# One store for the shift's last tokens, one page per unit, and stores moved to GpSimd's and ScalarE's queues

## The chip, the core and the metric

The kernel runs on one core of a Trainium2 chip. The metric is the device time of one execution, in microseconds (us). A core has TensorE (PE, with PEld for its weight loads), VectorE (DVE), ScalarE (ACT), GpSimd (POOL) and SyncE (SP). Each engine works through a queue of its own in order, and an instruction at the head of a queue that waits holds everything behind it. A DMA is issued by an instruction in the queue of SP, ACT or POOL and is then moved by 16 DMA engines, which all queues share.

## What is computed

One inference step of a hybrid decoder layer, for a prompt of 2048 new tokens and for 8 sampled sequences with 4096 cached positions each. After a modulated RMS norm, one projection makes the columns of two head groups. The first is sparse attention: an indexer scores all earlier positions, the best ones are attended. The second is RWKV-7 time mixing, whose columns pass a token shift before a delta-rule recurrence:

```
def rwkv_branch(xs, prev_row, S0, gate, mu_shift, ...):
    prev = jnp.concatenate([prev_row.astype(xs.dtype), xs[:, :-1]], axis=1)
    xm = xs + mu_shift * (prev - xs)
    r, k, v, wd, ad = jnp.split(xm, [...], axis=-1)
    ...
    S_new, y = wkv_scan(S0, rf, heads(decay), k_mod, vf, -kk, kk * a_h)
    ...
    return out.astype(xs.dtype), S_new, xs[:, -1:]
```

`xs[:, -1:]` is an output of its own, `shift_p`: the last token's 1664 projected columns, before the shift. The two groups' outputs are joined, projected once more and added to x. For the sampled sequences, the indexer's keys come from a paged cache: `cache_kidx[page_table]`, 32 pages of 128 positions for each of 8 sequences.

## The kernel before

The program is written against tiles in pools. A planner orders the instructions of all queues by a priority (the place in the program, shifted by `later(n)` by n places) and by a simulated timeline, allocates the buffers, and puts in every wait. `after(x, [y])` asks only that x stand behind y in that order. A tile with `bufs=1` has one buffer, so that its next user waits until every reader of the old content is done.

**Phase G** (`phase_g`) makes the projections of the prompt and runs the RWKV group. Tokens stand on the free axis in eight pieces of GT = 256. After a first part (norm, the "ad" columns in `g_ad`, the first gates in `g_ga`) comes a loop of 32 units k = (p, u): four pairs of heads p, eight token pieces u each. A unit passes through

- `front`: `g_front` multiplies the pair's columns r, k, v and gate (PE L196), copies them with scale to the tile `raw` (ACT L506) with one column for the token before, and mixes the shift (DVE L512). `raw` is a tile of 128 channels x 3 kinds x 257 columns with `bufs=1`; `g_pair` makes a new one for each pair and clears its column 0 (the memset of L489);
- `g_elem`: decays, keys and the like, on DVE and ACT;
- `g_chunk`: products within the pieces (L622, L627), then a round trip that turns small triangular blocks: eight stores asc<-UA (L643), eight loads As<-asc (L647), 15 steps of two GpSimd operations (L655, L656, Ut and Us), eight stores tsc<-Us (L658), one load TT<-tsc (L661);
- `g_inv` and `g_tail` take TT (first read by DVE L672), finish the inverse, run the recurrence (L770, L772), normalise, and store the result: ym is made by ACT (L813) and POOL (L814) and stored by SP to `mixd` (L815).

In iteration k the program has elem and chunk of unit k + 1, inv and tail of unit k, front of unit k + 2, then "filler" jobs (`a_job`, `g_ga`): matmuls that prepare the attention group (L204), whose queries are stored by SP from the tile `qo` (L872). Then `PG` steps of the generator `s_pages`, then `prefetch`, which loads the next weight tile (`load_w`: four loads wst of L178, each turned into two f16 halves by ACT L181 and DVE L182; `w` has four buffers) and, for some tiles, multiplies the sampled tokens' columns (`s_cols`), whose result `sat` is stored by SP (L341).

**The shift's last tokens.** The last column of `raw` after the last token piece is the output. In `g_front`, at u = 7, three stores (L518) write 128 floats each, one float from each partition; `g_ad` does so once (L469). That is 13 stores of 0.5 KB.

**The pages.** `s_pages` brings 32 groups of pages of the indexer's cache into a linear buffer `kxd`: an indirect gather issued by POOL (L1461) into the tile `pg` of 128 x 512 floats with `bufs=1`, and a store issued by SP (L1462). `PG = 2`: two of these steps per unit. `kxd` is read in phase A (`s_scores`, L1472).

**Phase A** (`phase_a`) loads K and V (L933, L934), scores, searches, attends and multiplies out, with the sampled sequences' work as background. Its instructions are in the same order plan; the loads have a priority of -3000.

Of the kernel before, what the change touches and what calls it, by code (L numbers as in the profile page):

```python
# [9 lines left out]
F32 = mybir.dt.float32  # L10
# [6 lines left out]
OP = mybir.AluOpType  # L17
# [14 lines left out]
GT = 256  # L32
# [8 lines left out]
class Kern:  # L41
# [166 lines left out]
    def phase_g(self):  # L208
        nc, V, A, G, PE, SY = self.nc, self.V, self.A, self.G, self.PE, self.SY
# [6 lines left out]
        with ExitStack() as es:  # L216
# [5 lines left out]
            bs = self.bs  # L222
# [24 lines left out]
            st, cx = {}, {}  # L247
# [55 lines left out]
            n = len(seq)  # L303
# [20 lines left out]
                prefetch()  # L324
            for _ in pages:
                pass
            self.A.activation(self.sg, self.sgr, AF.Tanh, scale=0.5)
            V.tensor_scalar(self.sg, self.sg, 0.5, 0.5, op0=OP.mult, op1=OP.add)
            V.tensor_tensor(self.sg, self.sg, self.sgr, op=OP.mult)

    def s_cols(self, name, w):

        c0 = {"q0": 0, "q1": 256, "kv": 512, "i0": 768, "i1": 1024, "ix": 1280}.get(name)
        if c0 is None:
            return
        ps = self.bank("e", 2)
        n = 72 if name == "ix" else 256
        self.gemm_n(ps[0:8, 0:n], self.hsl, w[:, :, :, 0:n])
        t = self.be.tile([8, 256], F32, name="sat", tag="bon", bufs=3)[:, 0:n]
        self.A.activation(t, ps[0:8, 0:n], AF.Copy, scale=1.0 / WS)  # L340
        self.SY.dma_start(self.sAd[:, c0:c0 + n], t)  # L341

    def gemm_u(self, u, w, dst):

# [15 lines left out]
    def consts_g(self, bs):  # L360
        V, SY = self.V, self.SY
        pb = self.pb
        P = lambda i: pb[:, 13 + 4 * i:17 + 4 * i]
        self.w0, self.a0, self.kk_w, self.ka, self.rk, self.lnw, self.lnb = (P(i) for i in range(7))
        dp = bs.tile([128, 5, 4], F32, name="dp")
        V.tensor_scalar(dp[:, 0], self.w0, 0.5, None, op0=OP.mult)
        V.tensor_scalar(dp[:, 1], self.a0, 0.5, None, op0=OP.mult)
        V.tensor_scalar(dp[:, 2], self.ka, 0.5, None, op0=OP.mult)
        V.tensor_scalar(dp[:, 3], self.ka, -0.5, 1.0, op0=OP.mult, op1=OP.add)
        V.tensor_scalar(dp[:, 4], self.kk_w, -0.5, None, op0=OP.mult)  # L370
        self.w0h, self.a0h, self.kah, self.kac, self.kkb = (dp[:, i] for i in range(5))

        self.RS = bs.tile([128, 2, 2, 2, 2], F32, name="RS")
        V.memset(self.RS, 1.0)
        self.omu = bs.tile([128, 13], F32, name="omu")
        V.tensor_scalar(self.omu, pb[:, 0:13], -1.0 / WS, 1.0 / WS, op0=OP.mult, op1=OP.add)

        self.lor = bs.tile([128, 4, 512], F16, name="lor")
        V.memset(self.lor[:, 2:4], 0.0)
        lo = self.a["lora"]  # L380
        for j in range(3):
            t = self.ap_.tile([128, 512], F32, name="lt", tag="nat", bufs=2)
            if j < 2:
                SY.dma_start(t, bass.AP(tensor=lo.tensor, offset=lo.offset + 64 * 512 * j, ap=[[0, 2], [512, 64], [1, 512]]))
            else:
                SY.dma_start(t, lo)
            if j < 2:
                self.A.activation(self.lor[:, j], t, AF.Copy, scale=WS)
                i = slice(64, 128)
                V.scalar_tensor_tensor(self.lor[i, j], t[i], WS, self.lor[i, j], op0=OP.mult, op1=OP.subtract)  # L390
            else:
                for n in range(2):
                    i = slice(64 * n, 64 * n + 64)
                    self.A.activation(self.lor[i, 2 + n], t[i], AF.Copy, scale=WS)

        self.wdad = self.dr.tile([128, 3, T], F16, name="wdad")
        self.raw12 = bs.tile([128, GT + 1], F32, name="raw12")
        V.memset(self.raw12[:, 0:1], 0.0)
        self.lwx = bs.tile([128, NCH, 65], F32, name="lwx")
        V.memset(self.lwx, 0.0)  # L400
        cg = bs.tile([128, CG_N], F32, name="cg")
        SY.dma_start(cg, self.a["cg"])
        self.cos = cg[:, 0:256].rearrange("p (i d) -> p i d", i=16)
        self.sin = cg[:, 256:512].rearrange("p (i d) -> p i d", i=16)
        self.wqk = bs.tile([128, 2, 64], F32, name="wqk")
        wq = self.a["wqk"]
        SY.dma_start(self.wqk.rearrange("p h d -> p (h d)"), bass.AP(tensor=wq.tensor, offset=wq.offset + 448, ap=[[0, 128], [1, 128]]))
# [41 lines left out]
    def g_ad(self, u, w):  # L449

        V, A, SY = self.V, self.A, self.SY
        sl = slice(u * GT, (u + 1) * GT)
        raw, out = self.raw12, self.be.tile([128, GT], F32, name="wo", tag="ta", bufs=1)
# [12 lines left out]
                SY.dma_start(self.wdad[64 * d:64 * d + 64, j, sl], hl[64 * j:64 * j + 64, 0])  # L466
        SY.dma_start(self.wdad[:, 2, sl], hl[:, 1])
        if u == T // GT - 1:
            SY.dma_start(self.a["o_shift_p"][12 * 128:13 * 128].rearrange("(p o) -> p o", o=1), raw[:, GT:])  # L469

    def g_ga(self, j, i, w):

# [19 lines left out]
    def g_front(self, st, u, w0, w1):  # L492
        nc, V, A, G, PE, SY = self.nc, self.V, self.A, self.G, self.PE, self.SY
        be = self.be
        p, raw = st["p"], st["raw"]
# [17 lines left out]
                if 2 * b + c0 + n == 4:  # L513
                    self.silu(gate, pg[:, (n - 1) * GT:])
        if u == T // GT - 1:
            for j in range(3):
                c0 = (4 * j + p) * 128
                SY.dma_start(self.a["o_shift_p"][c0:c0 + 128].rearrange("(p o) -> p o", o=1), raw[:, j, GT:])  # L518
        return dict(st=st, u=u, xm=xm, gate=gate, i=p * (T // GT) + u)

    def rsqrt(self, x):
# [86 lines left out]
    def g_chunk(self, cx):  # L608
# [20 lines left out]
        for s, src in ((2, BK.rearrange("p a s t -> p (a s) t")), (3, AV)):  # L629
            pt = self.bank("e", 2)  # L630
# [13 lines left out]
                         UA[16 * n:16 * n + 16, n // 4, :, :, 0, q:q + 16].rearrange("p a h t -> p (a h) t"))  # L644
        As = bv.tile([128, 16, 16], F32, name="As", bufs=2)
        for n in range(8):
            SY.dma_start(As[16 * n:16 * n + 16], bass.AP(tensor=asc.tensor, offset=asc.offset + 1024 * n,  # L647
                                                         ap=[[0, 4], [256, 4], [1, 256]]))
        Us = bv.tile([128, 4, 16], F32, name="Us", bufs=2)
        G.tensor_copy(Us, self.uinit)  # L650
# [1 line left out]
        for j in range(15):  # L652
            m, w = j // 4 + 1, 15 - j
            sh = [128, m, w]
            G.tensor_tensor(Ut[:, 0:m, j + 1:], bc(As[:, j:j + 1, j + 1:], sh), bc(Us[:, 0:m, j:j + 1], sh), op=OP.mult)  # L655
            G.tensor_tensor(Us[:, 0:m, j + 1:], Us[:, 0:m, j + 1:], Ut[:, 0:m, j + 1:], op=OP.add)  # L656
        for n in range(8):
            SY.dma_start(bass.AP(tensor=tsc.tensor, offset=tsc.offset + 16 * n * 256 + 16 * (n % 4),  # L658
                                 ap=[[256, 4], [64, 4], [1024, 4], [1, 16]]), Us[16 * n:16 * n + 16])
# [53 lines left out]
    def g_tail(self, cx):  # L713
# [98 lines left out]
        V.scalar_tensor_tensor(yc, yc, col(self.lnb), gate, op0=OP.add, op1=OP.mult)  # L812
        A.copy(ym[:, 0], yc)  # L813
        G.tensor_tensor(ym[:, 1], yc, ym[:, 0], op=OP.subtract)  # L814
        SY.dma_start(self.mixd[:, :, 4 + p, sl], ym)  # L815


    def a_job(self, kind, ip, w):
# [44 lines left out]
        if nh == 4:  # L863
# [5 lines left out]
            o = ap.tile([128, 2, 4, 128], F16, name="qo", tag="qo", bufs=2)  # L869
            A.copy(o.rearrange("p t h q -> p (t h q)"), pt)  # L870
            c = int(kind[1])
            SY.dma_start(self.qTd[kind[0] == "i"][:, 2 * ip:2 * ip + 2, 4 * c:4 * c + 4], o)  # L872
        else:
            if kind == "kv":
                SY.dma_start(tok(self.a["o_k_p"]), n3)
# [570 lines left out]
    def s_pages(self, p):  # L1446
# [11 lines left out]
        yield  # L1458
        for n in range(32):
            t = p.tile([128, 512], F32, name="pg", bufs=1)  # L1460
            G.indirect_dma_start(out=t, out_offset=None, in_=rows, in_offset=bass.IndirectOffsetOnAxis(ap=it[:, n:n + 1], axis=0))  # L1461
            SY.dma_start(self.kxd[n // 4, 8 * (n % 4):8 * (n % 4) + 8].rearrange("j (q d) k -> (j q) (d k)", q=16), t)  # L1462
            yield

    def s_scores(self, p):
        nc, V, A, G, PE, SY = self.nc, self.V, self.A, self.G, self.PE, self.SY
# [366 lines left out]
PB = 6  # L1833
P_LD = -3000
P_SC = 0
FILL = lambda k: 4 + (52 * (k + 1) + 28) // 29
F0, F1 = 1, 4
YB = 2
PG = 2
XTB, SQB = 3, 3  # L1840
X0 = 2
SQP = (0, 2)
# [217 lines left out]
```

## Time and profile before

| | us |
|---|---|
| median of 3 runs | 2457.18 |
| lowest, highest | 2455.85, 2461.61 |
| profiled execution | 2460.94 |
| its span, from first to last instruction | 2459.1 |
| unit loop, first asc store to last store of ym | 232.6 to 1464.1 |

The mean granted clock of TensorE is 0.925 of full speed. The chain of work that ended last is made up thus:

```profile
PE 33%; POOL 22%; DVE 11%; DMA 11%; issue 9%; SPq 7%; ACT 5%; POOLq 0%; DVEq 0%; ACTq 0%
```

A name with q is an engine's sequencer: an instruction that waits or issues a DMA while the engine proper does nothing. In the timeline, a row holds the start, the time taken, the engine, the line, the operation, the tiles written and read, the shapes, and in square brackets how long the engine had been idle and what ended that. In the list of waits a row holds who waited for what, the total, the times and the longest. In the view of one line, a row holds the count, then the shortest, median and longest duration in ns. SP only issues, so that its rows are issue times; where a DMA ends shows in who was released by it.

Two lists show what SP's own queue and POOL wait for most in the unit loop:

```profile
POOL Ut L655 <- DMA As<-asc: 217.7, 25, 23.2
```

```profile
SPq L658 <- POOL Us L656: 149.7, 28, 12.3
```

### The profile page before, as it was taken

The numbers are of one execution on the slowest core, as the hardware profiler recorded it, in microseconds if no ns is written. First come the engines' busy times: TensorE is split into PE (matmuls) and PEld (weight loads), VectorE is DVE, ScalarE is ACT, GpSimd is POOL, SyncE is SP. The second block draws the span as 40 slices with busy tenths as digits, with TensorE's granted clock in tenths as the row PEclk, the third lists the DMA queues.
The fourth block names the chain that finished last, engine by engine and source line by source line (L and its number), as shares of the span: only waits on it lengthen the run. The fifth ranks groups of instructions, "written<-read, shape, count | busy, mean of one in ns | idle before, by whom it ended". The sixth has DMA issues, their size and how long they took to land.

```text
span 2459.1 us, 55537 instructions
## 1 busy us (share of the span) xinstructions
PE 2108.7 (86%) x20799; PEld 1497.6 (61%) x20799; DVE 1611.1 (66%) x4998; ACT 1060.8 (43%) x2243; POOL 1097.0 (45%) x2841
## 2 busy tenths in 40 slices
PE   6788998699998999979998756998887789888997
PEld 1656777587776788868876432455555445455553
DVE  4883576586775766767876776867787744556531
ACT  1652223232332333322322345888767543665530
POOL 2311345334343243232343326357767765577722
PEclk9898999899999999989999676999889999998999
DMA  6435332311112211132111412312000033220133
GB/s 223 153 113 133 96 106 92 85 51 34 33 48 42 54 51 36 49 62 58 42 37 27 130 29 70 101 58 64 10 27 10 18 84 97 65 59 27 49 104 100
DMA packets 232537, 167.59 MB, mean 68 GB/s; under 512 B 108327, under 2 KB 193280, under 8 KB 232129
## 3 DMA queue, kind: packets, MB, share of 16 engines
q1 hardware_dynamic: 226817, 149.27, 21.8%
q0 software_dynamic: 3328, 10.49, 1.6%
q8 instruction: 165, 2.70, 0.5%
q10 hardware_dynamic: 2112, 4.19, 0.5%
q14 instruction: 115, 0.94, 0.1%
HBM read 113.87 MB, written 50.00 MB: 67 GB/s over the span
## 4 chain that ended last, share of the span: by engine, by line
PE 33%; POOL 22%; DVE 11%; DMA 11%; issue 9%; SPq 7%; ACT 5%; POOLq 0%; DVEq 0%; ACTq 0%
PE ps_g L196 8%; PE ps_s L1341 5%; SPq L647 3%; POOL Us L656 3%; POOL Ut L655 3%; PE ps_l L1031 3%; PE ps_v L1281 2%; PE ps_g L204 2%; PE ps_t L1273 2%; SPq L658 2%; PE ps_g L159 2%; ACT bias L1092 2%; DMA As<-asc 1%; DVE sc L1049 1%; PE ps_e L622 1%
## 5 line engine op out<-in xcount | busy, mean ns | idle before, releaser
L196 PE MATMUL ps_g<-h,w 128*128 128x256 f16 (+1 forms) x4032 | 512.0, 281 | 34.0 <-ACT sgr L356 8.1
L196 PEld LDWEIGHTS <-w 128*128 128x128 f16 x4032 | 394.7, 101 | 105.0 <-issue 31.2
L204 PE MATMUL ps_g<-w,h 128*128 128x256 f16 (+1 forms) x2304 | 251.8, 263 | 3.0 <-ACT nat L848 2.4
L655 POOL TENSOR_TENSOR Ut<-As,Us 128x12 f32<-128x12 f32 (+10 forms) x480 | 130.8, 273 | 260.1 <-DMA As<-asc 217.7
L1252 DVE CUSTOM_DVE_ANT_0 P<-ps_l,bias 128x1024 f32<-128x1024 f32 (+7 forms) x192 | 172.5, 908 | 106.2 <-PE ps_l L1031 61.4
L204 PEld LDWEIGHTS <-h 128*128 128x128 f16 (+1 forms) x2448 | 210.1, 99 | 35.9 <-issue 8.1
L1273 PE MATMUL ps_t<-cf,P 128*128 128x128 f32 x1088 | 185.3, 298 | 32.4 <-ACT P L1260 21.4
L1276 ACT COPY pT<-ps_t 128x512 f32<-128x512 f32 (+1 forms) x288 | 154.0, 560 | 128.7 <-PE ps_t L1273 125.3
L1049 DVE SCALAR_TENSOR_TENSOR sc<-r,wi,sc 128x1024 f32<-128x1024 f32 (+7 forms) x154 | 167.7, 1089 | 37.2 <-ACT r L1048 36.4
L1260 ACT ACTIVATE P<-P,mx 128x1024 f32<-128x1024 f32 (+7 forms) x192 | 171.5, 896 | 39.9 <-DVE mx L1258 39.6
L1273 PEld LDWEIGHTS ps_t<-cf,P 128*128 128x128 f32 x1088 | 130.0, 149 | 89.7 <-ACT P L1260 28.3
L1281 PE MATMUL ps_v<-pT,Vn 128*64 128x128 f32 x2176 | 162.7, 292 | 21.8 <-ACT pT L1276 21.2
L1341 PE MATMUL ps_s<-wo,mt 128*128 128x512 f16 x768 | 172.4, 379 | 7.8 <-DVE t L1345 6.3
L1048 ACT ACTIVATE r<-ps_l 128x1024 f32<-128x1024 f32 (+7 forms) x176 | 142.4, 816 | 76.4 <-PE ps_l L1031 48.5
L1031 PE MATMUL ps_l<-K,qiT 128*128 128x512 f16 (+3 forms) x608 | 154.9, 379 | 23.7 <-ACT r L1048 12.3
L1031 PE MATMUL ps_l<-K,qT 128*128 128x512 f16 (+3 forms) x640 | 155.4, 365 | 19.2 <-ACT r L1048 12.9
L1281 PEld LDWEIGHTS ps_v<-pT,Vn 128*64 128x64 f32 x2176 | 123.2, 143 | 70.3 <-ACT pT L1276 36.8
L1092 ACT ACTIVATE bias<-sc,sm 128x640 uint8<-128x640 f32 (+13 forms) x84 | 109.9, 1308 | 129.5 <-POOL sm L1123 113.3
L656 POOL TENSOR_TENSOR Us<-Us,Ut 128x12 f32<-128x12 f32 (+10 forms) x480 | 133.9, 279 | 34.7
L1341 PEld LDWEIGHTS <-mt 128*128 128x128 f16 x768 | 74.7, 98 | 96.0 <-issue 9.0
L1031 PEld LDWEIGHTS <-qT 128*128 128x128 f16 x640 | 64.7, 104 | 79.5 <-issue 40.8
L1031 PEld LDWEIGHTS <-qiT 128*128 128x128 f16 x608 | 61.6, 106 | 83.2 <-issue 48.9
(561 smaller groups left out, 4234.2 us busy)
## 6 DMA issues: line engine op xcount, KB each, us to landing
wst<-in_wt SPq DMA_DIRECT2D x60, 256.0 KB
xt<-in_xT SPq DMA_DIRECT2D x16, 512.0 KB
wa<-in_w_ada SPq DMA_DIRECT2D x8, 1024.0 KB
kxd<-pg SPq DMA_DIRECT2D x32, 256.0 KB
qTd<-qo SPq DMA_DIRECT2D x32, 256.0 KB
kx<-kxd SPq DMA_DIRECT2D x64, 128.0 KB
mt<-mixd SPq DMA_DIRECT2D x16, 512.0 KB
x<-in_x SPq DMA_DIRECT2D x32, 256.0 KB
```

The lines of the kernel that those rows point to most:

```text
L196: self.PE.matmul(out, w[:, a, k], h[:, b, k], start=(n == 0), stop=(n == 3 * KD - 1))
L204: self.PE.matmul(out, h[:, b, k], w[:, a, k], start=(n == 0), stop=(n == 3 * KD - 1))
L655: G.tensor_tensor(Ut[:, 0:m, j + 1:], bc(As[:, j:j + 1, j + 1:], sh), bc(Us[:, 0:m, j:j + 1], sh), op=OP.mult)
L656: G.tensor_tensor(Us[:, 0:m, j + 1:], Us[:, 0:m, j + 1:], Ut[:, 0:m, j + 1:], op=OP.add)
L1031: self.PE.matmul(ps[:, j:j + m], qs, self.K[:, kk, c0 + j:c0 + j + m], start=st, stop=not st)
L1049: self.dve = V.scalar_tensor_tensor(sc[:, c:c + n], r[:, :n], wi[:, h:h + 1], self.tz[:, c:c + n] if h == 0 else sc[:, c:c + n], op0=OP.mu ...
L1092: self.after(A.activation(ja[:, :L], sc[:, :L], AF.Sign, bias=t, accum_out=col(5)), [self.act])
L1252: self.dve = V.tensor_tensor_reduce(P[n][:, :w], pl[:, :w], bias[:, c:c + w], scale=1.0, scalar=-3.0e38, op0=OP.add, op1=OP.max, accum_out ...
L1260: self.act = A.activation(P[n][:, :w], P[n][:, :w], AF.Exp, scale=0.125, bias=mx[:, h, 2:3], accum_out=sums[:, n, h:h + 1])
L1273: PE.transpose(pt[:, q:q + 128], Ps[g][k // 8][:, k % 8 * 128:(k % 8 + 1) * 128], self.ident)
L1281: mm = PE.matmul(pv[64 * g:64 * g + 64, hh * 128:(hh + 1) * 128], self.Vn[:, k, 64 * g:64 * g + 64], pT[:, q + g * 128:q + g * 128 + 128], ...
L1341: PE.matmul(pg, mt[:, b, k], self.wo[:, a, k, js], start=(n == 0), stop=(n == 3 * KD - 1))
```

## The change

Four edits go together.

1. The 13 stores of single floats are replaced. A tile `shp` of 128 x 13 is filled by small DVE copies: one in `g_ad`, and one of three columns per pair in `g_front` (columns p, p + 4, p + 8). After the loop, with a priority moved 40 places ahead, a PE transpose turns it to 13 rows of 128, a DVE copy takes it to the tile `sho`, and one SP store writes 13 rows of 512 B.
2. `PG = 1`: one step of `s_pages` per unit. The gather must stand behind the last Us operation that has been written so far, the store of a page comes one step later and must stand behind the last As load written so far. The single buffer stays.
3. The store of `ym` is issued by POOL in place of SP.
4. The stores of `qo` and `sat` are issued by ACT in place of SP.

```diff
@@ phase_g, after the loop
             for _ in pages:
                 pass
+            with self.later(P_SH):
+                pt = self.bank("m", 2)
+                PE.transpose(pt[0:13, 0:128], self.shp, self.ident)
+                t = self.be.tile([13, 128], F32, name="sho", tag="So", bufs=1)
+                V.tensor_copy(t, pt[0:13, 0:128])
+                SY.dma_start(self.a["o_shift_p"].rearrange("(c p) -> c p", p=128), t)
@@ s_cols
-        self.SY.dma_start(self.sAd[:, c0:c0 + n], t)
+        self.A.dma_start(self.sAd[:, c0:c0 + n], t)
@@ consts_g
+        self.shp = bs.tile([128, 13], F32, name="shp")
@@ g_ad
         if u == T // GT - 1:
-            SY.dma_start(self.a["o_shift_p"][12 * 128:13 * 128].rearrange("(p o) -> p o", o=1), raw[:, GT:])
+            V.tensor_copy(self.shp[:, 12:13], raw[:, GT:])
@@ g_front
         if u == T // GT - 1:
-            for j in range(3):
-                c0 = (4 * j + p) * 128
-                SY.dma_start(self.a["o_shift_p"][c0:c0 + 128].rearrange("(p o) -> p o", o=1), raw[:, j, GT:])
+            V.tensor_copy(self.shp[:, p:p + 9:4], raw[:, :, GT])
@@ g_chunk
-            SY.dma_start(As[16 * n:16 * n + 16], ...
+            self.h_as = SY.dma_start(As[16 * n:16 * n + 16], ...
...
-            G.tensor_tensor(Us[:, 0:m, j + 1:], Us[:, 0:m, j + 1:], Ut[:, 0:m, j + 1:], op=OP.add)
+            self.h_us = G.tensor_tensor(Us[:, 0:m, j + 1:], Us[:, 0:m, j + 1:], Ut[:, 0:m, j + 1:], op=OP.add)
@@ g_tail
-        SY.dma_start(self.mixd[:, :, 4 + p, sl], ym)
+        G.dma_start(self.mixd[:, :, 4 + p, sl], ym)
@@ a_job
-            SY.dma_start(self.qTd[kind[0] == "i"][:, 2 * ip:2 * ip + 2, 4 * c:4 * c + 4], o)
+            A.dma_start(self.qTd[kind[0] == "i"][:, 2 * ip:2 * ip + 2, 4 * c:4 * c + 4], o)
@@ s_pages
         for n in range(32):
             t = p.tile([128, 512], F32, name="pg", bufs=1)
-            G.indirect_dma_start(out=t, ...)
-            SY.dma_start(self.kxd[...], t)
+            ld = G.indirect_dma_start(out=t, ...)
+            self.after(ld, [self.h_us])
             yield
+            st = SY.dma_start(self.kxd[...], t)
+            self.after(st, [self.h_as])
@@ constants
+P_SH = -40
-PG = 2
+PG = 1
```

More of the change, by code (lines that the diff above doesn't have):

```diff
@@ L646, in g_chunk @@
         for n in range(8):
-            SY.dma_start(As[16 * n:16 * n + 16], bass.AP(tensor=asc.tensor, offset=asc.offset + 1024 * n,
+            self.h_as = SY.dma_start(As[16 * n:16 * n + 16], bass.AP(tensor=asc.tensor, offset=asc.offset + 1024 * n,
                                                          ap=[[0, 4], [256, 4], [1, 256]]))
@@ L1460, in s_pages @@
             t = p.tile([128, 512], F32, name="pg", bufs=1)
-            G.indirect_dma_start(out=t, out_offset=None, in_=rows, in_offset=bass.IndirectOffsetOnAxis(ap=it[:, n:n + 1], axis=0))
-            SY.dma_start(self.kxd[n // 4, 8 * (n % 4):8 * (n % 4) + 8].rearrange("j (q d) k -> (j q) (d k)", q=16), t)
+            ld = G.indirect_dma_start(out=t, out_offset=None, in_=rows, in_offset=bass.IndirectOffsetOnAxis(ap=it[:, n:n + 1], axis=0))
+            self.after(ld, [self.h_us])
             yield
+            st = SY.dma_start(self.kxd[n // 4, 8 * (n % 4):8 * (n % 4) + 8].rearrange("j (q d) k -> (j q) (d k)", q=16), t)
+            self.after(st, [self.h_as])
     def s_scores(self, p):
```

## The prediction

> **What bounds the kernel now.** I read the page first, then the busy time by stage, then the timeline wherever TensorE stands still.
>
> ```profile
> span 2459.1 us, 55537 instructions
> PE 2108.7 (86%) x20799; PEld 1497.6 (61%) x20799; DVE 1611.1 (66%) x4998; ACT 1060.8 (43%) x2243; POOL 1097.0 (45%) x2841
> ```
>
> ```profile
> 340.00:470.00 130.00, 103.32 (x1153) 86.06 (x1153) 83.99 (x305) 37.65 (x95) 54.33 (x135) 0.88 0.35 93
> 470.00:600.00 130.00, 125.07 (x1527) 103.94 (x1527) 98.75 (x358) 45.33 (x109) 52.84 (x151) 1.00 0.18 48
> ...
> 800.00:1000.00 200.00, 195.98 (x2458) 162.04 (x2452) 139.29 (x453) 68.89 (x165) 73.10 (x217) 1.00 0.17 46
> ...
> 1345.00:1465.00 120.00, 77.76 (x825) 49.20 (x825) 84.39 (x247) 45.50 (x79) 30.01 (x78) 0.74 0.28 82
> ```
>
> The columns are: stretch, length, busy time of PE, PEld, DVE, ACT, POOL, then granted clock, DMA share, GB/s. The unit loop runs from about 230 to 1465 us. From 800 to 1000 PE is busy for 196 of 200 us while DVE has 139, POOL 73 and ACT 69: PE is the bound there, so what counts is time in which PE stands. Over 340 to 470 it stands for 26.7 us, over 470 to 600 for 4.9. The long stops, found in the timeline, are five, and each has a store of the shift's last tokens just before it:
>
> ```profile
> 206.00 0.46 SPq L469 DMA_DIRECT2D out_shift_p<-raw  x1
> 206.54 0.39 SPq L178 DMA_DIRECT2D wst<-in_wt  x1
> 216.07 0.63 ACT L181 ACTIVATE w<-wst 128x512 f16<-128x512 f32 x1 [10.10 <-DMA wst<-in_wt]
> 216.75 0.61 PE L196 MATMUL ps_g<-h,w 128*128 128x256 f16 x2 [8.14 <-ACT sgr L356]
> ...
> 457.89 0.63 ACT L181 ACTIVATE w<-wst 128x512 f16<-128x512 f32 x1 [12.76 <-DMA wst<-in_wt]
> 458.85 0.64 PE L708 MATMUL ps_t<-TT,g 32*32 32x32 f32 x16 [13.47 <-ACT g L704]
> ...
> 793.46 0.42 DVE L795 TENSOR_REDUCE gx<-ps_m 128x4 f32<-128x256 f32 x1 [14.37 <-DMA out_shift_p<-raw]
> 794.55 0.64 PE L708 MATMUL ps_t<-TT,g 32*32 32x32 f32 x16 [11.56 <-ACT g L704]
> ...
> 1087.27 0.16 DVE L530 SCALAR_TENSOR_TENSOR gx<-gx 128x4 f32<-128x4 f32 x1 [12.04 <-DMA out_shift_p<-raw]
> 1089.27 0.43 PE L680 MATMUL ps_t<-tr,UA 16*32 16x32 f32 x14 [10.86 <-DVE ko L889]
> ...
> 1344.36 0.33 SPq L661 DMA_DIRECT2D TT<-tsc  x1
> 1353.94 0.45 DVE L672 STREAM_TRANSPOSE tr<-TT 128x256 f32<-128x256 f32 x1 [12.43 <-DMA TT<-tsc]
> 1354.44 0.53 PE L680 MATMUL ps_t<-tr,UA 16*32 16x32 f32 x18 [11.53 <-DVE tr L672]
> ```
>
> PE idles 8.14 + 13.47 + 11.56 + 10.86 + 11.53 = 55.6 us here. Two things meet. DVE sits behind the memset of the next pair's `raw` (L489): `raw` has one buffer, and the memset must wait until the stores have read it:
>
> ```profile
> L518 SPq DMA_DIRECT2D out_shift_p<-raw x12: 357/389/1062, 431.9 to 1343.2; - x12
> ...
>   DVE gx L795: 14.4, 1
>   DVE gx L530: 12.0, 1
> ```
>
> And everything else on the DMA engines crawls at the same time:
>
> ```profile
> 219.00:229.00 10.00, 9.69 (x61) 6.66 (x59) 3.80 (x8) 2.83 (x6) 1.48 (x2) 0.72 0.64 206
> ...
> 784.00:794.00 10.00, 0.00 (x0) 0.00 (x0) 0.51 (x3) 0.00 (x0) 6.55 (x30) 0.69 0.90 34
> ...
> 1344.00:1350.00 6.00, 0.00 (x0) 0.00 (x0) 0.00 (x0) 0.00 (x0) 0.24 (x1) 0.79 0.43 51
> ```
>
> At 784 the engines are 90% busy and move 34 GB/s; over 219 to 229 they are 64% busy and move 206. So the weight tile (L178 to L181) or the TT load (L661 to L672) that happens to be under way lands late too.
>
> **The change part by part.** *The shift stores.* Thirteen stores of 128 single floats go. In their place stand five small DVE copies into `shp`, and near the loop's end one transpose, one copy and one store of 13 rows of 512 B. Not all of the 55.6 us returns, for something is late next. At 206 the weight load, issued at 206.5, would still need some 2.9 us (the landing of a tsc store, quoted with the rivals), so ACT resumes near 209.5 instead of 216.1: 6.6 us. At 445 SP itself was late (the pages, below), so I leave 2 us: 11.5. At 783 and 1078 DVE simply goes on: 11.0 and 10.5. At 1343 TT would land 2.9 us after its issue at 1344.4, not 9.6 after it: 6.6, rounded down. Sum 46.2 us.
>
> After four of the stops PE also runs at half clock:
>
> ```profile
> 216.00:224.00 8.00, 6.09 (x27) 3.72 (x28) 2.70 (x5) 2.83 (x7) 0.97 (x1) 0.50 0.68 188
> ...
> sum 31.00, PE 23.20 PEld 16.65 DVE 19.82 ACT 12.09 POOL 4.87; mean PE 5.80 PEld 4.16 DVE 4.95 ACT 3.02 POOL 1.22
> ```
>
> These are four stretches (216 to 224, 459 to 470, 795 to 798, 1089 to 1098), all at 0.50. PE's 23.2 us there would take half: 11.6 us. After the fifth stop the work is a serial chain, and I count nothing.
>
> What is added:
>
> ```profile
> L500 DVE COPY raw<-raw x28: 105/169/630, 124.8 to 1317.0; 128x3 f32<-128x3 f32 x28
> ```
>
> Five copies at 0.17 us, and a transpose and one more copy that I put at 0.3 each (an estimate: less than the 0.53 us of PE's L680 burst and the 0.45 us of DVE's L672 above): 1.5 us if nothing hides them. They can hide, except in the last units, where PE has no filler. I take +1.5; the ends are 0 and, should the extra use of a "m" bank hold the last units' chain, +3. The new store's landing is waited for by nothing.
>
> *The pages.* Before, two pages per unit in program order, and the planner pulled them ahead: 32 in 189 to 463 us.
>
> ```profile
> L1461 POOL DMA_INDIRECT pg<-in_kidxT,pgi x32: 943/990/1514, 189.0 to 463.4; - x32
> ```
>
> ```profile
> POOL pg L1461 <- DMA kxd<-pg: 80.6, 20, 12.8
> ...
> SPq L1462 <- DMA pg<-in_kidxT,pgi: 87.4, 21, 7.1
> ```
>
> One page buffer means that POOL waits for each store and SP for each gather, 81 and 87 us in all. Afterwards a gather stands behind its unit's Us chain and its store behind the next unit's As loads, so both find their data long there. What queues behind those two now is the UA to TT round trip (L643 to L661). Its cost to PE shows only over 340 to 470: 26.7 of idle, less the 13.5 counted, less the 4.9 that the next 130 us have too, leaves 8.3 us. I take half, 4 us, with 0 and 8.3 as ends. In return some 25 units carry one gather of 0.99 us on POOL, which is 36% busy there, and 512 KB of traffic at a DMA share of 0.17: nothing, at most a third of 25 us.
>
> *The queues.*
>
> ```profile
> L815 SPq DMA_DIRECT2D mixd<-ym x32: 535/573/612, 319.3 to 1464.1; - x32
> ```
>
> ```profile
> L872 SPq DMA_DIRECT2D qTd<-qo x32: 365/383/1547, 376.0 to 1025.2; - x32
> ```
>
> ```profile
> L153 ACTq DMA_DIRECT2D wa<-in_w_ada x4: 374/374/428, 3.1 to 12.1; - x4
> ```
>
> ```profile
> POOL ym L814 <- ACT ym L813: 147.8, 20, 30.1
> ```
>
> SP sheds 32 x 0.573 + 32 x 0.383 + six small ones (under 2 us): 32 us of issue, plus its waits for `ym` and `qo`, behind which asc, As, tsc and TT queue. ACT takes on 38 issues at about 0.37: 14 us on an engine 34% busy. POOL takes on 32 stores. No plain store of POOL's is in the trace; the nearest row is the gather, 0.94 to 1.51 us, so 30 to 48 us, and I take 32. POOL idles 147.8 us just before `ym` alone, so this fits. For PE I take 0, with a gain of 5 and a loss of 15 as ends.
>
> The Trainium skill, "SBUF — State Buffer", section "A bandwidth-pool intuition that's wrong (but worth ruling out)", says that a DMA issued from GpSimd waits for its descriptors while VectorE holds the port that both share, some 620 ns becoming 3100. By that page POOL would lose 32 x 2.5 = 79 us more, as an estimate, and the sum below would still stand if its idle time took them. The gathers' 1.5 us at most, beside a DVE 70% busy, shows a part of it at the most.
>
> *Sum*, on the profiled execution's own time of 2460.9 (its span and 1.8 around it): 2460.9 - 46.2 - 11.6 - 4 + 1.5 = **2401 us**. That execution lies 3.8 above the median of 2457.2; I don't take them off, since the planner lays the whole loop out anew and small new waits are more likely than none. From 1465 on nothing is touched; it only starts earlier.
>
> **The rivals.**
>
> *The stores are not the source.* Then the crawl belongs to the weight loads that come at each pair's end, and only the memset's wait goes. Of the gains 11.0 and 10.5 stay, with about 5 of half clock: 2461 - 27 = **2434**. For it: three of the five stops end with a weight or TT landing, not with L489. Against it: the crawl at 1344 has no weight load near, and the chain holds
>
> ```profile
> 607.91 2.93 DMA tsc<-Us
> ```
>
> ```profile
> 1078.45 8.66 DMA out_shift_p<-raw
> ```
>
> as a tsc store, in runs of 16 floats, against one of single floats. The Trainium skill, "DMA: Bandwidth & Descriptors", section "Specifications", puts the border at 512 B, below which the DMA engine reads, modifies and writes. By that rule alone the 512 tiny asc and tsc stores, in 64 B runs, would crawl too, and taking 13 stores out would be worth little; the 2.93 against 8.66 speaks for the single floats as a case of their own.
>
> *More comes back.* In the tail unit 30's As loads wait behind the next phase's K loads:
>
> ```profile
> 1351.34 0.59 SPq L933 DMA_DIRECT2D K<-Kd  x1
> ...
> 1365.74 4.08 SPq L647 DMA_DIRECT2D As<-asc  x4
> ```
>
> If the new order puts them after the As loads, another 14 us of those 120 with PE at 78 may go: **2386**, and with the pages' other half and the queues' 5, 2377.
>
> *GpSimd falls behind.* If every `ym` store takes the longest gather's 1.51 us and stands ahead of a Us chain that PE needs, 32 x 1.51 = 48 us come back: **2448**. POOL's idle time speaks against it.
>
> *Slower: ScalarE is held in its queue.* The trace has ACT issue DMAs only at the start, and there it stood until landings that the waiting work does not use:
>
> ```profile
> 12.60 0.63 ACT L424 ACTIVATE sq<-xt 128x512 f32<-128x512 f32 x1 [5.97 <-DMA ct<-in_cT]
> ```
>
> L424 does not read `ct`; ACT's load, in the queue ahead of it, was held for a landing of SP's. If the 38 new issues are each held so, until an SP store that is itself late, 38 x 6 = 227 us of ACT are lost in front of the copies that free `ps_g` (L506, L511). Two banks cover a hold of some 6 us (48 matmuls at 0.13); holds beyond that reach PE. It decides from 68 us on PE, say twelve holds of 12 us: 2461 - 61 + 75 = **2475**. Against it: ACT has most of its time free, and a `qo` is issued once in 20 us.
>
> **How the numbers follow.** A measurement of this kernel can tell about 0.3%, 7.4 us, from no change. Forecast 2401 (2386 to 2420): 0.52. Stores not the source, about 2434: 0.24. More comes back, 2372 to 2386: 0.12. GpSimd behind, 2448, just inside 0.3%: 0.05. Slower, 2475: 0.07. So faster 0.88, same 0.05, slower 0.07. The range 2372 to 2446 leaves out the last two.
>
> **What would show it.** Right: no PE stop over 8 us between 200 and 1300; no DMA share near 0.9 at under 80 GB/s; L489 released by DVE alone; 32 gathers about one unit apart, with hardly any POOL wait on kxd; the unit loop's end near 1405. Wrong: stops at the four pair ends again, now on wst (first rival); idle time of ACT before L506 or the copies of L356 that ends with a landing (the slower one); Ut waiting longer on As although SP is freed (GpSimd).

## The result and the profile after

The changed kernel takes 2383.22 us (median of 4 runs, 2375.97 to 2385.84) against 2456.51 us (4 runs, 2455.55 to 2461.61): the ratio is 0.9693, with a 95% interval of 0.9667 to 0.9719. It is faster by 73 us; 56 to 60 were forecast. Its profiled execution took 2385.06 us. The page of the changed kernel:

```profile
span 2383.3 us, 55550 instructions
PE 2089.7 (88%) x20800; PEld 1487.3 (62%) x20800; DVE 1607.7 (67%) x5004; ACT 1060.0 (44%) x2243; POOL 1140.0 (48%) x2873
```

To see where the time went I cut the span at the end of the last operation that writes `ym`, which is the end of the unit loop (phase A follows); what is called the loop from here on is all that stands before this cut, the first part of the kernel included. The view of busy time by stretch, of the changed kernel and then of the kernel before; its columns are stretch, length, busy time of PE, PEld, DVE, ACT, POOL, granted clock, DMA share and GB/s:

```profile
0.00:1390.60 1390.60, 1259.95 (x14713) 999.90 (x14713) 1003.06 (x3340) 487.38 (x1172) 529.07 (x1399) 0.95 0.27 79
1390.60:2383.30 992.70, 829.71 (x6087) 487.42 (x6087) 604.66 (x1665) 572.64 (x1071) 610.94 (x1476) 0.91 0.20 59
```

```profile
0.00:1464.10 1464.10, 1276.83 (x14712) 1009.88 (x14712) 1005.02 (x3334) 488.46 (x1172) 491.66 (x1368) 0.93 0.27 75
1464.10:2459.10 995.00, 831.84 (x6087) 487.70 (x6087) 606.06 (x1665) 572.38 (x1071) 605.32 (x1474) 0.92 0.20 59
```

PE carries out the same matmuls up to the loop's end (14,713; the one more is the transpose of `shp`). So the loop's length splits into PE's busy time, which for the same matmuls is shorter where the granted clock is higher (0.95 after, 0.93 before), and PE's idle time, which is the length less the busy time. The loop lost 73.5 us: 56.6 of idle time (187.3 to 130.7) and 16.9 of busy time. Phase A lost 2.3.

Four of the five long stops are gone. The view of PE's waits in the changed kernel, from 200 to 1267 us (waiting group, what it waited for, us in total, times, the longest):

```profile
PE ps_g L196 <- ACT xm L518: 5.7, 3, 2.5
...
PE ps_t L892 <- POOL HL L885: 4.0, 4, 1.9
...
PE ps_t L692 <- DVE g L687: 2.7, 1, 2.7
```

Nothing there is above 2.7 us, where before four stops were 8 to 13.5. The fifth stood in the last units, and there PE still waits for what comes of the TT load. The same view from 1267 to 1391 us:

```profile
PE ps_t L685 <- DVE tr L677: 15.1, 2, 7.8
```

These are two stops of 7.8 and 7.4 us; before, they were 11.5 (the fifth stop) and 7.9. The stretches just after the five copies into `shp`, in the changed kernel:

```profile
204.00:214.00 10.00, 7.25 (x64) 5.91 (x63) 5.03 (x10) 5.03 (x13) 0.67 (x1) 1.00 0.44 126
418.00:428.00 10.00, 7.61 (x74) 6.06 (x73) 9.83 (x40) 3.49 (x11) 2.88 (x6) 0.76 0.27 80
733.00:743.00 10.00, 10.00 (x145) 8.29 (x142) 6.33 (x23) 3.55 (x9) 5.93 (x23) 1.00 0.46 137
1008.00:1018.00 10.00, 10.00 (x129) 8.79 (x127) 5.97 (x27) 2.40 (x8) 3.55 (x14) 1.00 0.42 133
1268.00:1278.00 10.00, 8.02 (x136) 6.69 (x134) 8.19 (x36) 2.70 (x9) 0.36 (x2) 0.92 0.41 110
```

The DMA engines are busy for 27 to 46% and move 80 to 137 GB/s; before it was 90% at 34. From 200 us to the loop's end, cut into stretches of 5 us, the changed kernel has none in which the engines are over 60% busy and move less than 80 GB/s; the kernel before has four, from 210, 450, 785 and 1080 us on, each behind a group of the stores. The pages, by the view of the tile `pg` of the changed kernel (line, engine, operation, tile, count: ns at least/median/most, first and last start; then idle time before them):

```profile
L1466 POOL DMA_INDIRECT pg<-in_kidxT,pgi x32: 1009/1051/1328, 276.3 to 1345.4; - x32
...
  DMA kxd<-pg: 4.3, 1
```

They are spread over the whole loop as forecast, and POOL's 80.6 us of waiting for `kxd` are down to 4.3. The view also puts 10.7 us of a Us chain's wait down to the landing of a page; Ut (L660) reads no page, and the eight As loads that it does read were issued just before that page's store, so this is a wait for As. POOL's new stores of `ym`, by the view of their line in the changed kernel:

```profile
L820 POOL DMA_DIRECT2D mixd<-ym x32: 687/724/768, 305.7 to 1391.4; - x32
...
DMA to landing us min/median/max: 2.2/2.3/4.4
```

One costs POOL 0.72 us, below the 0.94 to 1.51 between which the prediction had put it.

### The profile page after: what moved, and what is told of

Read it like the earlier page. It is cut to its first block, busy times and chain, and to the rows that moved or that the text cites. A ratio compares the mean times of both kernels' runs of the same rounds, so it can differ in the third digit from the quotient of the medians.

```text
span 2383.3 us, 55550 instructions
## 1 busy us (share of the span) xinstructions
PE 2089.7 (88%) x20800; PEld 1487.3 (62%) x20800; DVE 1607.7 (67%) x5004; ACT 1060.0 (44%) x2243; POOL 1140.0 (48%) x2873
## 4 chain that ended last, share of the span: by engine, by line
PE 35%; POOL 24%; DVE 12%; issue 9%; DMA 7%; SPq 7%; ACT 5%; POOLq 0%; ACTq 0%; DVEq 0%
PE ps_g L196 8%; PE ps_s L1346 5%; POOL Us L661 4%; PE ps_g L204 3%; POOL Ut L660 3%; PE ps_l L1036 3%; SPq L652 3%; PE ps_v L1286 2%; PE ps_t L1278 2%; PE ps_g L159 2%; SPq L663 2%; DMA As<-asc 1%; PE ps_e L627 1%; ACT bias L1097 1%; SPq L648 1%
## 5 line engine op out<-in xcount | busy, mean ns | idle before, releaser
L196 PE MATMUL ps_g<-h,w 128*128 128x256 f16 (+1 forms) x4032 | 506.0, 279 | 29.3 <-ACT h L453 6.9
L660 POOL TENSOR_TENSOR Ut<-As,Us 128x12 f32<-128x12 f32 (+10 forms) x480 | 133.5, 278 | 313.4 <-DMA As<-asc 265.4
L1278 PE MATMUL ps_t<-cf,P 128*128 128x128 f32 x1088 | 184.1, 296 | 21.1 <-ACT P L1265 13.5
L1346 PE MATMUL ps_s<-wo,mt 128*128 128x512 f16 x768 | 179.4, 389 | 11.0 <-DVE t L1350 5.6
L1036 PE MATMUL ps_l<-K,qT 128*128 128x512 f16 (+3 forms) x640 | 153.1, 364 | 25.8 <-ACT r L1053 14.8
L661 POOL TENSOR_TENSOR Us<-Us,Ut 128x12 f32<-128x12 f32 (+10 forms) x480 | 143.6, 299 | 34.6
L1097 ACT ACTIVATE bias<-sc,sm 128x2048 uint8<-128x2048 f32 (+13 forms) x84 | 109.9, 1308 | 106.8 <-POOL sm L1128 96.3
```

The lines of the kernel that those rows point to most:

```text
L196: self.PE.matmul(out, w[:, a, k], h[:, b, k], start=(n == 0), stop=(n == 3 * KD - 1))
L661: self.h_us = G.tensor_tensor(Us[:, 0:m, j + 1:], Us[:, 0:m, j + 1:], Ut[:, 0:m, j + 1:], op=OP.add)
L1036: self.PE.matmul(ps[:, j:j + m], qs, self.K[:, kk, c0 + j:c0 + j + m], start=st, stop=not st)
L1278: PE.transpose(pt[:, q:q + 128], Ps[g][k // 8][:, k % 8 * 128:(k % 8 + 1) * 128], self.ident)
L1346: PE.matmul(pg, mt[:, b, k], self.wo[:, a, k, js], start=(n == 0), stop=(n == 3 * KD - 1))
```

## The experiments

All results first. Loop, PE busy, PE idle and rest (the span after the loop's end) are from each kernel's profiled execution, cut as above. Each ratio is to the kernel before as it ran in the same batch, with medians of 2449.3 to 2457.9 us. Two pairs of kernels with the very same order of work differ little: the changed kernel and e12 by 1.5 us in the loop, e9 and e13 by 5.2. But the runs of one kernel spread by 6 us (e12) to 24 (e13), and the profiled one was the fastest of e1's, 7.3 us below their median, and the slowest of e2's, e3's, e9's, e12's and e13's, 3.3 to 12.5 above it. So a difference between two rows is good to some ten us where no other pair bears it out. The matmuls in the loop are 14,712 or 14,713 in every row.

| kernel | parts of the change | median us | ratio, 95% interval | loop | PE busy | PE idle | rest |
|---|---|---|---|---|---|---|---|
| before | none | 2456.5 | | 1464.1 | 1276.8 | 187.3 | 995.0 |
| changed | all | 2383.2 | 0.9693 (0.9667 to 0.9719) | 1390.6 | 1260.0 | 130.7 | 992.7 |
| e1 | shift | 2384.5 | 0.9730 (0.9704 to 0.9756) | 1405.2 | 1264.0 | 141.2 | 970.1 |
| e2 | pages | 2419.5 | 0.9859 (0.9839 to 0.9880) | 1450.3 | 1281.1 | 169.2 | 972.2 |
| e3 | queues | 2461.1 | 1.0023 (1.0005 to 1.0040) | 1474.4 | 1286.2 | 188.2 | 991.7 |
| e8 | shift, queues | 2386.6 | 0.9717 (0.9694 to 0.9739) | 1401.7 | 1265.2 | 136.5 | 981.5 |
| e9 | shift, pages | 2373.3 | 0.9656 (0.9631 to 0.9681) | 1399.6 | 1271.2 | 128.4 | 977.1 |
| e10 | pages, queues | 2393.2 | 0.9774 (0.9747 to 0.9800) | 1426.0 | 1274.7 | 151.3 | 966.5 |
| e5 | all, floats stored from `shp` | 2419.1 | 0.9849 (0.9814 to 0.9884) | 1434.8 | 1274.5 | 160.3 | 983.0 |
| e6 | all, and floats 256 B apart | 2368.8 | 0.9646 (0.9610 to 0.9682) | 1398.0 | 1266.7 | 131.3 | 968.2 |
| e7 | all, and floats side by side | 2411.6 | 0.9814 (0.9791 to 0.9837) | 1439.2 | 1283.2 | 156.0 | 972.4 |
| e11 | all, and 21 small stores | 2394.2 (one run) | | 1413.5 | 1275.9 | 137.6 | 978.8 |
| e12 | all, `P_SH` 0 | 2383.4 | 0.9724 (0.9708 to 0.9741) | 1392.1 | 1262.6 | 129.5 | 992.7 |
| e13 | shift, pages, `P_SH` 0 | 2372.1 | 0.9666 (0.9638 to 0.9694) | 1404.8 | 1272.4 | 132.4 | 978.0 |

**One part at a time (e1, e2, e3).** Each puts one part of the diff shown above into the kernel before: e1 the shift (the five copies, the transpose and the row store), e2 the pages (`PG = 1`, the late store, the two orders), e3 the three stores' queues.

> The kernel before with only the shift's last tokens stored once as rows; pages and queues as they were. Theory (the single-float stores carry the gain): the prediction's terms for them, 46.2 + 11.6 - 1.5 = 56 us, so about 2400, and none of the five long PE stops, but the POOL and SP waits of the pages (81 and 87 us) still there. If the 17 us by which the changed kernel beat the forecast belong to the stores too: about 2383. Rival (pages and queues carry much of it): 2420 to 2440.

> The kernel before with only the pages' part: one page per unit, stored a unit later. Theory: 4 us less than before (0 to 8), about 2452, with the five stops still there. Rival (the pages carry the 17 us that the forecast missed): about 2440. POOL's wait on kxd nearly gone in either case.

> The kernel before with only the queues' part: ym stored by GpSimd, qo and sat by ScalarE. Theory: no difference, within 8 us of 2457, since PE is the bound and waits for none of these stores. Rival (SP freed of waits shortens the asc to TT round trip): 10 to 17 us less, about 2443. Other rival (ScalarE held in its queue): 2465 or more, with idle time of ACT before the issue.

The shift alone shortens the loop by 58.9 us: 46.1 of PE's idle time and 12.8 of its busy time. This is read from two single executions that lie 83.8 us apart, while the medians of that batch lie 68.3 apart, so it is rather too much. By the medians the shift alone is as fast as the whole change, 2384.5 and 2383.2: what the other two parts take off the loop, phase A's 992.7 us after e1's 970.1 give back. Pages alone shorten it by 13.8, with 18.1 less idle time and 4.3 more busy time; the median falls by 33, more than the loop gives, since the rest is 22.8 us shorter in that kernel although nothing of phase A is edited; 2419.5 is far below both of its expectations. Queues alone lengthen the loop by 10.3, nearly all of it busy time (9.4), and the ratio is just above 1; the median is within the 8 us of 2457 that were expected, and 8.3 above the kernel before in its own batch.

**The floats without the memset's wait (e5).** The changed kernel, but the thirteen stores of single floats stay; they read `shp`, so the memset of `raw` needn't wait for them. The row store and its transpose go. This was to part the two causes that met in the stops.

```diff
             V.tensor_copy(self.shp[:, p:p + 9:4], raw[:, :, GT])
+            for j in range(3):
+                c0 = (4 * j + p) * 128
+                SY.dma_start(self.a["o_shift_p"][c0:c0 + 128].rearrange("(p o) -> p o", o=1), self.shp[:, 4 * j + p:4 * j + p + 1])
```

> The changed kernel, but the 13 stores of single floats stay: they read the tile shp, so that the memset of the next raw waits for no store. Theory (single floats make the DMA engines crawl, and that alone stops PE): stops stay where a weight or TT load lands late; with about 25 us of stops and 8 of half clock, about 2415, and DMA share near 0.9 at under 80 GB/s behind each store. Rival (the memset's wait was the whole harm): the same as the changed kernel, 2383. Rival (the crawl belongs to the weight loads at the pair ends and needs no float store): 2383 too, but then the crawl is in the changed kernel's trace as well.

The stores alone, with no memset behind them, cost 29.6 us of idle time and 14.6 of busy time in the loop against the changed kernel. So the stores seem to be a source by themselves, but the order of the work is another too, a cause that the next pair rules out.

**Is it the number of stores or where their floats land (e6, e7)?** The changed kernel with thirteen more stores of 128 single floats from `shp` to a scratch tensor in HBM, issued where e5 has its own. In e6 the floats land 256 B apart, in e7 side by side. Nothing else differs: in the two traces every engine has the same order from the first instruction to the last.

```diff
+        self.scr = self.dr.tile([13, 128, 64], F32, name="scr")
...
+            for j in range(3):
+                SY.dma_start(self.scr[4 * j + p, :, 0:1], self.shp[:, 4 * j + p:4 * j + p + 1])
```

For e7 the tile is `[13, 128]` and the target `self.scr[4 * j + p].rearrange("(p o) -> p o", o=1)`.

> The changed kernel, plus 13 stores of 128 single floats each from shp into a scratch buffer in HBM, where the floats lie 256 B apart; nothing waits for them. Theory (neighbouring single floats in one row of 512 B hinder each other, and so the DMA engines crawl): no crawl here, 2383 to 2388. Rival (any store of single floats makes the engines crawl): as with the floats taken from shp, 33 to 44 us more than the changed kernel, about 2420.

> The changed kernel, plus the same 13 stores of 128 single floats, into a scratch buffer where the 128 floats lie side by side. Theory and rival of the floats apart both: the crawl is back, 33 to 44 us more than the changed kernel, about 2420, with DMA share near 0.9 at under 80 GB/s behind each. If it stays at 2383, the crawl hangs on the output tensor or on the place in the order, not on the store's form.

The busy time of the stretches at the last store of each of the five groups, first in e6, then in e7 (columns as before, the last two being DMA share and GB/s):

```profile
203.50:211.50 8.00, 5.96 (x52) 4.74 (x50) 3.78 (x8) 3.69 (x10) 0.67 (x1) 1.00 0.49 135
418.00:428.00 10.00, 7.81 (x66) 5.32 (x65) 8.02 (x30) 2.62 (x9) 1.55 (x5) 0.67 0.14 31
733.00:743.00 10.00, 10.00 (x152) 8.45 (x151) 6.33 (x25) 3.48 (x10) 6.92 (x28) 1.00 0.46 135
1018.00:1028.00 10.00, 10.00 (x183) 8.39 (x182) 6.46 (x37) 1.75 (x5) 3.20 (x15) 1.00 0.37 108
1298.00:1308.00 10.00, 9.31 (x62) 6.59 (x60) 7.34 (x19) 3.81 (x7) 1.36 (x2) 0.71 0.84 285
```

```profile
201.00:209.00 8.00, 4.85 (x44) 3.99 (x41) 2.39 (x5) 2.05 (x6) 0.67 (x1) 0.97 0.87 36
422.00:432.00 10.00, 8.08 (x67) 5.53 (x65) 8.19 (x32) 2.75 (x9) 1.51 (x5) 0.67 0.22 31
741.00:751.00 10.00, 7.32 (x119) 5.98 (x119) 2.99 (x11) 1.22 (x4) 6.50 (x30) 1.00 0.45 52
1043.00:1053.00 10.00, 2.59 (x54) 1.90 (x52) 0.65 (x4) 0.00 (x0) 3.50 (x16) 0.76 0.82 79
1330.00:1340.00 10.00, 6.88 (x46) 4.69 (x42) 3.49 (x10) 1.88 (x3) 0.63 (x1) 0.75 0.89 32
```

Side by side, the engines are 87% busy for 36 GB/s and 89% for 32; 256 B apart, 49% for 135 and 84% for 285. At 1043 PE works for 2.59 of 10 us in e7 and at 1018 all the time in e6; only at the second group do the two hardly differ. The whole kernel differs by 43 us, the loop by 41.2: 24.6 of idle and 16.6 of busy time. Against the changed kernel, whose order is another, e6 has 0.7 us more of idle time and 6.7 of busy time. So neither such stores as such nor the size of their pieces makes the engines crawl, but that the floats lie side by side.

The Trainium skill, "DMA: Bandwidth & Descriptors", section "Specifications", says that a DMA engine reads, modifies and writes whatever is below 512 B. Both kernels write the same 4-byte pieces, so a rule by size alone gives them the same time; the 43 us between them decide that something else is at work.

**How far apart is enough (e11).** The changed kernel with seven groups of three stores of 128 floats each, issued by POOL, with another spacing in each group: 4, 16, 64 and 256 B at the ends of the four pairs, 8, 32 and 128 B in the fourth unit of the first three.

```diff
+    def spaced(self, n, t, c):
...
+        flat = lambda j, e: bass.AP(tensor=self.scr.tensor, offset=self.scr.offset + (3 * n + j) * 16384, ap=[[e, 128], [1, 1]])
...
+            if n == 0:
+                G.dma_start(flat(j, 1), s)
+            if n == 1:
+                G.dma_start(flat(j, 4), s)
```

> The changed kernel plus seven groups of three stores of 128 single floats into scratch, issued by GpSimd so that their landings show, the floats 4, 8, 16, 32, 64, 128 and 256 B apart. Theory (writes into the same short stretch of HBM wait for one another): landings of 6 us or more at 4 B, falling with the spacing, and near 2.3 us (that of ym) from some spacing of 32 to 128 B on. Rival (only whole 512 B rows matter): still slow at 128 B, where four floats share a row. The time itself says little: two to four slow groups, some 10 to 25 us more.

Each spacing has a line of its own, so the view of that line gives the time from issue to landing. Lines 539, 541, 549 and 543 are 4, 16, 32 and 64 B:

```profile
L539 POOL DMA_DIRECT2D scr<-shp x3: 538/560/621, 427.8 to 429.0; - x3
...
DMA to landing us min/median/max: 7.6/8.1/15.8
...
L541 POOL DMA_DIRECT2D scr<-shp x3: 538/545/562, 754.5 to 755.6; - x3
...
DMA to landing us min/median/max: 6.5/6.9/7.3
...
L549 POOL DMA_DIRECT2D scr<-shq x3: 538/545/572, 609.3 to 610.3; - x3
...
DMA to landing us min/median/max: 1.7/1.7/1.7
...
L543 POOL DMA_DIRECT2D scr<-shp x3: 540/540/577, 1034.5 to 1035.6; - x3
...
DMA to landing us min/median/max: 1.7/1.7/1.8
```

The other three landed after 3.0 to 10.1 us (8 B), 1.8 to 3.8 (128 B) and 3.5 to 4.0 (256 B). Each spacing was seen at one place and in one execution, beside whatever else the engines did there. The 8 and the 64 B groups stand alike, both issued just as SP began its eight As loads: 3.0 to 10.1 us against 1.7 to 1.8. The 16 B group had a page store and weight loads issued right beside it, so its 6.9 us need not be its own. Behind the 4 B group the engines crawl as soon as weight loads join; behind the 16 B group they don't:

```profile
435.00:445.00 10.00, 7.83 (x60) 5.93 (x53) 5.38 (x15) 1.04 (x3) 2.54 (x3) 0.66 0.90 27
754.00:764.00 10.00, 9.60 (x142) 8.11 (x141) 3.68 (x13) 2.38 (x7) 7.26 (x27) 1.00 0.53 88
```

So the border lies somewhere between 8 and 32 B. A border at whole rows of 512 B has fallen. Mine, from 32 to 128 B, holds at its lower end, but the 128 and 256 B groups stayed above the 2.3 us expected, and why is not shown. The one run took 2394.2 us, 11 more than the changed kernel, as expected.

**Two parts at a time (e8, e9, e10).** The changed kernel without the pages (e8), without the queues (e9), and without the shift (e10, whose floats are stored from `raw` as before).

> The changed kernel without the pages' part (two pages per unit, stored at once). By the end of the unit loop the pages alone gave 14 us, the shift 59, the queues -10. If parts add up: unit loop's end near 1415 and about 2395 to 2400. If the pages gave their 14 us only by getting out of the way of the shift's stop at 445: loop's end near 1400 to 1405, as with the shift alone.

> The changed kernel without the queues' part (SP issues ym, qo and sat). If parts add up and the queues cost 10 us: unit loop's end near 1381 to 1390, and 2370 to 2383. Rival (with the stops gone the freed SP queue is worth the 17 us that the forecast missed): loop's end near 1400 to 1405, about 2395.

> The changed kernel with the shift's 13 stores as before, read from raw (pages and queues changed). Set beside the run that reads them from shp (2419): if the crawl is nearly all the harm, within 6 us of it, the memset's wait costing little. If the memset's wait is a good part, 10 to 25 us more, 2430 to 2445, with DVE stopped for over 8 us before it at pair ends.

Once the stores are gone, the pages take 12.8 us of idle time away (e1 to e9; 8.8 to e13) and the queues 4.7 (e1 to e8) with nothing more on top of the pages (e9 to the changed kernel, 2.2 us added). e8's loop ends at 1401.7, as with the shift alone, which is the second of its expectations; e9 has the time of its first (2373.3) with nearly the loop of its rival (1399.6); e10, 2393.2, lies below both of its own. e10 and e5 both keep the thirteen stores; e10 keeps the memset's wait too, and yet its loop is 8.8 us shorter than e5's, all of it idle time, though DVE stood there for 21.1 us in two stops that ended with a store's landing. So no cost of the memset's wait by itself came out of this. But the three stores of a pair stand together in e5 and apart in e10, and the order of the loop is another: what the wait was worth stays open.

**The same order, placed otherwise (e12, e13).** The changed kernel and e9 with the new transpose at another due time, which changes none of the work.

```diff
-P_SH = -40
+P_SH = 0
```

> The changed kernel with one number altered, the priority of the block that stores the shift (0 in place of -40), which by itself is worth nothing. Theory (the planner's new layout of everything after it moves the time by up to 12 us either way): somewhere in 2368 to 2396, the unit loop's end within 8 us of 1391, the difference in phase A. Rival (layout is worth nothing): 2383 within 4.

> Shift and pages without the queues' part, and again the priority 0 in place of -40. Theory (the queues' part is worth nothing or costs a little): with the run at -40 (2373) below the changed kernel's two, so 2365 to 2380. Rival (2373 was the luck of one layout): 2380 to 2395.

The expectation that any such number gives another layout fell: the planner wrote the same order for all engines, and the times came back, 2383.4 for 2383.2 and 2372.1 for 2373.3. That makes the rest of the kernel a matter of order rather than of chance: 992.7 twice, 977.1 and 978.0, and 968.2 and 972.4 in e6 and e7, which share one too. Other orders of the same phase A lie between 966.5 and 995.0. Between the changed kernel and e9, PE's order in phase A differs at 3,852 of 6,087 matmuls.

e13, the shift and the pages without the queues, is the better version: 0.9666 (0.9638 to 0.9694) beside e12's 0.9724 (0.9708 to 0.9741), timed on one chip, 11 us less. e6 is lower still, at 2368.8, though it does more work than the changed kernel: its phase A, in another order, took 968.2 us against 992.7.

## Why the prediction was right, and where its size was off

The forecast was 60.3 us off the profiled execution of 2460.9; 75.8 came off. Term by term, from the profiled executions:

| term of the sum | forecast | measured | from |
|---|---|---|---|
| stores, less the added work: PE's idle time | 44.7 | 46.1 | before to e1 |
| half clock after the stops: busy time | 11.6 | 12.8 | before to e1 |
| pages and queues: idle time | 4 | 10.5 | e1 to changed |
| pages and queues: busy time | 0 | 4.1 | e1 to changed |
| after the loop | 0 | 2.3 | before to changed |

**The stores were right** in kind, and so was the half clock; in size they agree within what one execution of each kernel can tell, and e1's was a fast one. Of the signs named, there is no stop over 8 us between 200 and 1300, no crawl, and no wait of the memset (now L496). "The unit loop's end near 1405" is where e1, the stores alone, ends: 1405.2; the changed kernel's ends at 1390.6. Each of the five stops was charged with what would be late next, not with its whole length. Cut at nearly the same matmuls, e1 has 8.7 us less idle time up to the loop's start (first stop, 6.6 forecast), 13.2 in the first units (second stop, 11.5), 20.6 in the middle (third and fourth, 21.5) and 3.5 in the last four units (fifth, 6.6 less the 1.5 added).

The cause was right as well, but the runs make it sharper. The prediction set single floats against runs of 64 B; e6 and e7 show that single floats crawl only as neighbours. The rival in which the stores are not the source (2434) falls with e7, which takes 43 us more than e6 in the same order, and with e5, 36 us above the changed kernel. The memset's wait alone has not been priced.

**The pages were mis-sized.** The step was: "Its cost to PE shows only over 340 to 470 ... I take half, 4 us, with 0 and 8.3 as ends." With the stores gone, the cost can be seen by itself. Busy time by stretch in e1 (all pages early), then in e9 (one page per unit):

```profile
224.00:260.00 36.00, 34.83 (x346) 29.91 (x344) 15.76 (x46) 8.14 (x20) 12.14 (x35) 1.00 0.36 110
260.00:300.00 40.00, 38.53 (x483) 31.68 (x482) 22.17 (x75) 9.33 (x26) 13.16 (x40) 0.96 0.31 91
300.00:340.00 40.00, 36.60 (x459) 29.09 (x458) 28.63 (x94) 12.99 (x36) 15.96 (x43) 0.96 0.39 112
```

```profile
224.00:260.00 36.00, 36.00 (x401) 31.34 (x399) 16.58 (x50) 9.23 (x24) 8.35 (x31) 1.00 0.15 41
260.00:300.00 40.00, 39.86 (x493) 32.62 (x492) 27.83 (x96) 12.11 (x34) 15.82 (x49) 1.00 0.19 54
300.00:340.00 40.00, 38.15 (x454) 30.88 (x454) 27.15 (x90) 12.16 (x33) 14.30 (x49) 0.96 0.28 75
```

PE idles 6.0 us here in e1 and 2.0 in e9: 4 us, all before 340, where I had looked for none. From 340 to 500 it is 14.8 against 9.2, another 5.6. In all, e9 has 9.6 us less idle time and 99 matmuls more in these 276 us. So the loss was spread, 1.2 to 2.2 us in six of the seven slices of 36 to 40 us; I subtracted the idle time of a later stretch and halved the rest. In e1 the waits themselves are still there, by the view of waits from 180 to 500 us:

```profile
POOL pg L1466 <- DMA kxd<-pg: 58.2, 19, 6.2
```

In the changed kernel none of this line is left in that stretch. The parts also overlap: pages alone take 18.1 us of idle time and the shift 46.1, together 56.9 on the mean of e9 and e13, not 64.2. The prediction met this once, where it left 2 us at 445 because SP was late with pages.

**The queues were right at nothing** for PE's idle time: 0.9 us more alone, 4.7 less or 2.2 more beside the others, all within what one execution can tell. What they do to PE's busy time is not settled. Alone they add 9.4 us of it, beside the shift 1.2, and beside the shift and the pages they take some 10 away (1271.2 and 1272.4 without them, 1260.0 and 1262.6 with them), for the same matmuls; the granted clock to the loop's end is 0.94 without and 0.95 with them. But the executions of e9 and e13 read here are the slowest of their four. Phase A is 15 us longer with the queues (992.7 against 977.1 and 978.0) and the medians differ by 10 to 11, so at the medians some 4 to 5 us of gain in the loop are left, as an estimate from these numbers. **"From 1465 on nothing is touched; it only starts earlier"** came out within 2.3 us, and that was luck: without an edit there, the rest of the kernel took 966.5 to 995.0 us in the kernels of the table, by their order, and the order that the change got happens to be nearly as long as the one before. In e1 it gave 24.9 us that no term had. What in an order costs the time was not traced.

**The other rivals.** GpSimd falling behind (2448) rested on 1.51 us for a store; it was 0.72, and POOL's busy time rose from 1097.0 to 1140.0. PE's waits for POOL, all for the tile HL, are 4.4 us up to 1267, against 6.4 up to the same place before. The sign named for this rival did show: Ut waits longer for As, 265.4 us against 217.7. But e1, where the queues are as before, has 263.5, so the new stores are not its source. (2448 would also have been 9 us under the median before, a little more than the 7.4 us that the prediction called inside.) The Trainium skill, "SBUF — State Buffer", section "A bandwidth-pool intuition that's wrong (but worth ruling out)", would have a DMA issued from GpSimd take 3100 ns beside a VectorE copy in place of 620. The 32 stores held POOL for 687 to 768 ns and landed 2.2 to 4.4 us after issue, beside a DVE that is busy for 72% of the loop, so a loss of 2.5 us on each isn't seen here. ScalarE held in its queue (2475): apart from the weight tiles that it reads, ACT waits for landings for 3.1 us in all in the changed kernel's loop, and e3, the queues alone, costs at most 10 us by the median's interval. More coming back in the tail: the last four units, cut at the ends of `ym`, took as long as before, in the changed kernel and then in the kernel before it:

```profile
1267.10:1390.60 123.50, 85.08 (x892) 54.60 (x889) 87.75 (x255) 47.74 (x86) 41.99 (x84) 0.76 0.31 97
```

```profile
1339.30:1464.10 124.80, 81.37 (x857) 52.22 (x856) 85.70 (x248) 46.90 (x83) 29.48 (x78) 0.75 0.27 80
```

Of the 6.6 us that I counted for the fifth stop, none shows in the length. PE's idle time there fell from 43.4 to 38.4 us, but 35 more matmuls stand in that stretch. In e1's sum the other four stops make up for it. The half clock stood after the fifth stop too (1354 to 1381 us before, 23.5 us of PE's work at 0.50); the prediction counted nothing for it, and a matmul of these last units takes as long on average as before, 0.095 us.

## What to carry to other kernels

A transfer of many small pieces is judged by where the pieces land: side by side they can hold up everything else on the DMA engines, so gather them on the chip and store whole rows, or keep them apart (256 B was enough in e6; 32 and 64 B landed fast in the one execution of e11). When a stop goes, charge it with what is late next; when a wait is spread over many units, add up the idle time of all of them and not of the worst stretch. In a planned kernel, cut the span at the edge of what was edited and read each side by itself, PE's idle time apart from its busy time: a new order alone moved the untouched side by more than two of the three parts were worth.

## What the hardware showed that was not expected

128 floats stored 4 B apart took 7.6 to 15.8 us to land in e11, 32 B apart 1.7 us, and other loads on the same engines were slowed as well: 32 GB/s at 89% busy beside neighbouring floats in e7. Where between 8 and 32 B the border lies, and what is behind it, these runs don't show. The clock made up a good part of the cost: of the 41.2 us that neighbouring floats cost in e7's loop, 16.6 were PE's busy time for the same matmuls in the same order, at a granted clock of 0.93 against e6's 0.94.
